# The attention branch's projection of an encoder layer as seven block products for each pair of column tiles

## The chip, the core and the metric

The kernel runs on one core of one Trainium2 chip. The metric is the device time of one execution in microseconds (us). Three runs of the kernel before gave 2049.7, 2049.95 and 2050.43 us; the median is 2049.95. The engines are TensorE (PE; its weight loads are listed as PEld), VectorE (DVE), ScalarE (ACT), GpSimd (POOL) and SyncE (SP). POOL and SP issue the transfers here.

## The reference, cut to what matters

One encoder layer on 1024 tokens of 1024 channels: a SwiGLU FFN with a layer norm, a mixer with a layer norm, and a second FFN with a layer norm. The mixer's end is what changes:

```
g_attn = gates[..., :D_MODEL]
g_four = gates[..., D_MODEL:]
merged = g_attn * (attn @ w_proj_attn) + g_four * (four @ w_proj_fourier)
return merged @ w_out
```

`attn` is (1024 tokens, 512), `w_proj_attn` is (512, 1024). The product `attn @ w_proj_attn` is the attention branch's projection.

## The kernel before, in words

**Number format.** A float32 operand x is held as two tiles: hi, x rounded to the matmul's input format by an ACT copy, and lo, x minus hi on DVE (`split`, L352; the two instructions are L358 and L363). A product takes three matmuls, hi·hi, hi·lo and lo·hi (`TERMS`), into one PSUM bank of 128x512 float32. There are eight banks. SBUF pages are 128x1024 float32, 46 of them; half pages 128x512, eleven.

**Seven block products.** The large products of the kernel are done in 2x2 blocks with seven block products instead of eight. With the operand's blocks a11 to a22 and the weight's b11 to b22 the kernel forms

```
s1 = a21 - a22   s3 = a11 - a21   s2 = s1 - a11   s4 = a12 + s2
t1 = b11 + b12   t2 = t1 + b22    t3 = b12 + b22  t4 = t2 + b21
PROD = {1: ("a11", "b11"), 2: ("a12", "b21"), 3: ("s4", "b22"), 4: ("a22", "t4"),
        5: ("s1", "t1"), 6: ("s2", "t2"), 7: ("s3", "t3")}
```

Class `Operand` (L411) holds an operand's blocks: `derive` makes the sums on DVE (L473, L476, L479, L482) and splits each of the seven left factors; `mms` (L492) issues a block product's matmuls. A block product with four inner tiles is twelve matmuls. The banks are shared: bank A collects products 1 and 2, bank B begins as a copy of A after product 1 and collects 6, 7 and 4, bank D collects 5 and 3. Between the products ACT copies B away and DVE forms differences, so that the four output blocks come out of three banks.

**The plan.** Class `Flow` orders the whole kernel when it is built. `job` gives PE's work in a fixed order, each with a cost from `MM = 0.2267` us for one matmul of 128x512. `V`, `S` and `G` are DVE, ACT and POOL steps with costs, a job that needs them and a lead; `Q` are loads; `F` are small PE floats that are put between jobs when they are ready. `Flow.run` walks through the jobs and gives each engine's next instruction by these costs, by due times and by free banks and pages. What comes out is one fixed order for each engine; on the chip, semaphores keep the order between engines, and each engine works in its own order.

**The stage around the change** comes between the gate products (the last pairs `s20` and `s21`, PE line L495, tiles As and Ds) and the output projection (`WJ`, L2214, tiles wA, wB, wD). It holds:

- the four attention tiles of 128 inner rows by 1024 tokens, stored by `combine` (L1870) in `attn_d`, loaded into `at` (L1943, SP) and split into `ap0` to `ap3`;
- the projection `PJ[c]` for eight column tiles c (`run`, L2125, tile pj): four inner tiles by three terms by two halves of tokens, 24 matmuls into two banks, then on DVE the product with the gate tile `gl` out of both banks (L2133);
- the weights `wpa`, prepared and stored earlier by `keep_parts` (L1751; loads L1806), loaded again as hi and lo at L1778;
- the Fourier branch: channel products `fc` (L1965), their parts `fold` (L1976 on ACT, L1981 on DVE), position sums `fse`, `fp`, `fsem`, `fpm` (L2035, L2006, L2067), from whose banks the parts are taken on ACT and DVE: sine halves `fsp` (L2049, L2053), cosine parts `fch` and `fcl` (L2013 to L2019), edge terms `f_se` (L2024, L2025), middle terms `fmidT` (the same lines with four rows, and L2076), the middle weights `wm` (L2097 on ACT, L2098 on DVE); then `FJ[c]` for eight column tiles (L2151 to L2159, tiles pfe, pfo, pfs; three banks each), after which ACT takes the sine half `pfq` (L2166) and DVE forms the outputs (L2173 to L2177), the product with the gate (L2180) and the sum with the attention branch (L2189, tile ma), which is the output projection's operand `M` (`X4`).

The order of PE's jobs is given by `branch_jobs` (L1729): PJ 0 to 4, FJ 0 and 1, PJ 5, FJ 2 and 3, PJ 6, FJ 4 and 5, the first output-projection job, FJ 6, PJ 7, FJ 7, and the rest of the output projection.

Of the kernel before, what the change touches and what calls it, by code (L numbers as in the profile page):

```python
# [12 lines left out]
AF = mybir.ActivationFunctionType  # L13
# [3 lines left out]
P = 128  # L17
S0 = 1024
D = 1024
# [55 lines left out]
class Flow:  # L75
# [232 lines left out]
def kernel(  # L308
# [14 lines left out]
    def as_k(t, kd=KD):  # L323
        return t.rearrange("p (k n) -> p k n", k=kd)
# [86 lines left out]
    class Operand:  # L411


        def __init__(self, name):
            self.name = name
            self.raw, self.part, self.node, self.got = {}, {}, {}, {}

        def cols(self, n, kind, k):
            return pick(self.part[n, k // 2], kind)[:, (k % 2) * 512:(k % 2) * 512 + 512]

        def nodes(self, n):
            return [self.node[n, i] for i in range(2)]

        def turn(self, m, node, tile_of, c0, slack=4.0):

# [27 lines left out]
        def derive(self, first, whole, lead):  # L453

            raw, got = self.raw, self.got

            def parts(n, i, deps, need, src=None, gives=0, tokens=False):
                self.node[n, i] = split(f"{self.name}{n}{i}", lambda: raw[src or n, i],
                                        lambda p: self.part.__setitem__((n, i), p), deps, need,
                                        lead if need is first.get(n) else 14.0, gives=gives, tokens=tokens)  # L460
                return self.node[n, i]
            for n in ("a11", "a12", "a21", "a22"):
                for i in range(2 if first[n] else 0):
# [6 lines left out]
            for i in range(2):  # L470
# [12 lines left out]
                v1 = V(1.23, s1, got["a21", i] + got["a22", i], whole[6], lead + 6, 6.0, pages=1)  # L483
                v3 = V(1.23, s3, [v1, self.node.get(("a21", i), [])] + list(got["a11", i]), whole[6], lead + 5, 5.0)
                v2 = V(1.23, s2, [v3, self.node["a11", i]], whole[6], lead + 4, 4.0)
                parts("s2", i, [v2], whole[6], "a11", 1)
                parts("s3", i, [v3], whole[7], "a21", 1)
                parts("s1", i, [v1], whole[5], None, 2)
                v4 = V(1.23, s4, [v2, self.node["a12", i]], whole[3], lead + 3, 3.0)
                parts("s4", i, [v4], whole[3], "a12", 1)  # L490

        def mms(self, out, w, xn, first, last):  # L492
            for k in range(4):
                for ti, (a, b) in enumerate(TERMS):
                    nc.tensor.matmul(out, pick(w, a)[:, k * P:(k + 1) * P], self.cols(xn, b, k),  # L495
                                     start=first and k == 0 and ti == 0, stop=last and k == 3 and ti == 2,
                                     skip_group_check=True)


# [1226 lines left out]


    PJ, FJ, WJ = {}, {}, {}
    def branch_jobs(attn_, four_):  # L1729
        for c in attn_:  # L1730
            PJ[c] = job(24 * MM, None, 2, gives=(2 if c % 2 else 0) + (8 if c == 7 else 0))
        for c in four_:
            FJ[c] = job(3.1, None, 3, gives=(2 if c % 2 else 0) + (8 if c == 7 else 0))
    branch_jobs((0, 1, 2, 3, 4), (0, 1))
    branch_jobs((5,), (2, 3))
    branch_jobs((6,), (4, 5))
    WORDER = ((1, "A", True), (2, "A", False), (6, "B", False), (7, "B", False), (5, "D", True), (4, "B", False),
              (3, "D", False))
    for p, bk, new in WORDER:
        for m in range(4):  # L1740
            WJ[p, m] = job(12 * MM, None, int(new), gives=8 if m == 3 else 0)
            if (p, m) == (1, 0):
                branch_jobs((), (6,))
                branch_jobs((7,), (7,))

    root_table(FJ[0])


# [53 lines left out]
    for c2 in range(4):  # L1802
        cs = slice(c2 * 256, (c2 + 1) * 256)

        def load_pa(t, cs=cs):
            nc.sync.dma_start(as_k(t, 4), w_pa.rearrange("(k p) n -> p k n", p=P)[:, :, cs])  # L1806
# [61 lines left out]
    attn = {}  # L1868

    def combine(h):  # L1870

# [41 lines left out]
        for hf in range(2):  # L1913
# [25 lines left out]
            T["n", hf] = an  # L1939

        def load():
            T["a"] = t = page(f"at{h}")
            nc.sync.dma_start(t, attn_d[h])  # L1943
        q = Q(PJ[0], 0.5, load, [(T["n", 0], 5.0), (T["n", 1], 5.0)], 26.0, pages=1)
        split(f"ap{h}", lambda: T["a"], lambda p: attn.__setitem__(h, p), [q], PJ[0], 30.0)

    for h in range(SLOTS):
        combine(h)
# [161 lines left out]
        return Q(need, 0.5, run, [(gate_n[w, c], 5.0)], pages=1)  # L2110

    pj_n, seeds = {}, {}
    for c in range(8):
        c2, cc = divmod(c, 2)
        st = {}
        if cc == 0:
            kept["a", c2](("a", c2), PJ[c], 28.0)

        def run(c=c, c2=c2, cc=cc, st=st):
            st["b"] = bk = [bank(f"pj{c}{hf}") for hf in range(2)]  # L2120
            wv = [as_k(t, 4) for t in PW["a", c2]]
            for k in range(4):
                for ti, (a, b) in enumerate(TERMS):
                    for hf in range(2):
                        nc.tensor.matmul(bk[hf], pick(wv, a)[:, k, cc * P:(cc + 1) * P],  # L2125
                                         pick(attn[k], b)[:, hf * 512:(hf + 1) * 512],
                                         start=(k == 0 and ti == 0), stop=(k == 3 and ti == 2))
        PJ[c].fn = run
        q = gate_load(0, c, PJ[c])

        def mul(hf, c=c, st=st):
            t = gates[0, c][:, hf * 512:(hf + 1) * 512]
            nc.vector.tensor_mul(t, t, st["b"][hf])  # L2133
        pj_n[c] = [V(0.69, lambda hf=hf, mul=mul: mul(hf), [PJ[c], q], frees=1) for hf in range(2)]

    for c in range(8):
        c2, cc = divmod(c, 2)
        st = {}
# [25 lines left out]
        def sine(c=c, st=st):  # L2164
            st["q"] = half(f"pfq{c}")
            nc.scalar.activation(st["q"], st["s"], AF.Copy)  # L2166
            if c > 5:
                seeds[c - 6][0] = st["s"]

        def outs(c=c, st=st):  # L2170
            pe, po, q = st["e"], st["o"], st["q"]
# [19 lines left out]
        n = S(0.62, sine, [FJ[c]], frees=int(c < 6), halves=1)  # L2191
        if c > 5:
            seeds[c - 6] = [None, n]
        n = V(1.8, outs, [n], frees=2, hgives=1, pages=1)
        n = V(1.23, gate, [n, q], gives=1)
        n = V(1.38, merge, [n] + pj_n[c], gives=2, pages=2 if cc == 0 else 0)
        for r in (1, 2):
            X4.got.setdefault((f"a{r}{c // 4 + 1}", c % 4 // 2), []).append(n)

# [189 lines left out]
```

## Time and profile before

| what | value |
|---|---|
| median of three runs | 2049.95 us (2049.7 to 2050.43) |
| profiled execution: span from the first to the last instruction | 2048.2 us |
| what lies around the span, median less span | 1.75 us |
| instructions | 25801 |
| from the first pj matmul to the end of FJ 7 | 1255.7 to 1342.1 us |
| DMA moved over the whole span | 442.23 MB |

The profiled execution lists no time of its own beside its span; the median of the runs stands for it. In the profile's lists a group names line, engine, operation, written tile and read tiles; "x24" is a count. In a timeline the columns are start, length, engine, line, operation, tiles, shape, and in brackets how long the engine had been idle before it and what ended the idle time. The matmuls of a timeline overlap, so that the distance between starts, not the length, is what one costs. The chain that ended last is followed back from the last instruction. A list of waits gives the waiting engine and line, what it waited for, the sum, the count and the longest.

### The profile page before, as it was taken

How to read it: one execution, taken by the hardware profiler on the slowest of the kernel's cores; microseconds unless marked ns; L12 is line 12 of the kernel's file. 1: busy time of each engine (PE TensorE's matmuls, PEld its weight loads, DVE VectorE, ACT ScalarE, POOL GpSimd, SP SyncE). 2: the span in 40 equal slices, each digit the busy share in tenths (PEclk: the TensorE clock that was granted, in tenths of full speed). 3: DMA queues.
4: the chain of work that ended last, by engine and by line, in shares of the span. 5: the costliest groups of instructions: out<-in, count | busy, mean ns of one | idle time of the engine just before them, and what ended most of it. 6: DMA issues, size and time to landing. Idle time of an engine off the chain costs nothing.

```text
span 2048.2 us, 25801 instructions
## 1 busy us (share of the span) xinstructions
PE 2037.5 (99%) x9411; PEld 1700.3 (83%) x9411; DVE 1339.6 (65%) x1930; ACT 893.6 (44%) x1417; POOL 266.9 (13%) x464
## 2 busy tenths in 40 slices
PE   9999999999999999999999999999999999999998
PEld 7888888888888888888888888888888888888886
DVE  7765555576685668665656664777876665575565
ACT  6433333454453224665556443236633333355332
POOL 0122211111001122231121110000011111110000
PEclk9999999999999999999999999999999999999999
DMA  5778875599856566564455659574257886658752
GB/s 206 237 236 259 257 230 148 171 339 402 291 189 187 178 228 212 195 207 147 117 142 169 232 209 373 183 297 175 78 179 238 272 243 205 194 205 292 238 184 94
DMA packets 164144, 442.23 MB, mean 216 GB/s; under 512 B 20370, under 2 KB 42722, under 8 KB 163504
## 3 DMA queue, kind: packets, MB, share of 16 engines
q1 hardware_dynamic: 118928, 288.41, 40.7%
q0 software_dynamic: 45088, 152.16, 25.1%
q8 instruction: 74, 1.21, 0.2%
q14 instruction: 54, 0.44, 0.1%
HBM read 329.63 MB, written 176.91 MB: 247 GB/s over the span
## 4 chain that ended last, share of the span: by engine, by line
PE 98%; DMA 1%; ACT 1%; DVE 0%; issue 0%; SPq 0%; DVEq 0%
PE Ab L495 14%; PE Aa L495 14%; PE Aq L495 8%; PE Db L495 6%; PE Da L495 6%; PE As L495 5%; PE Dq L495 3%; PE Xb L864 3%; PE Xa L864 3%; PE Zb L864 3%; PE Za L864 3%; PE pj L2125 2%; PE v L1291 2%; PE Ds L495 2%; PE wA L2214 2%; PE vB L1230 2%
## 5 line engine op out<-in xcount | busy, mean ns | idle before, releaser
L1621 ACT ACTIVATE p<-p,stat 128x192 f32<-128x192 f32 (+2 forms) x96 | 42.2, 441 | 29.7 <-DVE stat L1616 27.7
L338 POOL DMA_DIRECT2D hsaa<-t2a x21 | 12.0, 569 | 316.0 <-DVE t2a L730 297.9
L338 POOL DMA_DIRECT2D n_spill<-y x16 | 9.0, 565 | 297.5 <-DVE y L1061 297.5
L338 POOL DMA_DIRECT2D hsba<-t2b x21 | 11.6, 550 | 265.4 <-DVE t2b L730 253.6
L726 DVE TENSOR_TENSOR t2a<-Da,t2a 128x512 f32<-128x512 f32 x21 | 14.5, 691 | 45.2 <-PE Da L495 45.2
L633 ACT ACTIVATE t2b<-Ab 128x512 f32<-128x512 f32 x21 | 12.6, 598 | 63.8 <-PE Ab L495 63.8
L726 DVE TENSOR_TENSOR t2b<-Db,t2b 128x512 f32<-128x512 f32 x21 | 14.5, 691 | 39.1 <-PE Db L495 39.1
L633 ACT ACTIVATE t2a<-Aa 128x512 f32<-128x512 f32 x21 | 12.5, 598 | 62.5 <-PE Aa L495 62.5
L1411 DVE SCALAR_TENSOR_TENSOR oq<-Dq,b_cols,t2q 128x512 f32<-128x512 f32 x12 | 11.8, 985 | 41.2 <-PE Dq L495 41.2
L1606 DVE SCALAR_TENSOR_TENSOR p<-sc,bias 128x512 f32<-128x512 f32 (+1 forms) x40 | 24.4, 619 | 17.9 <-PE sc L1592 17.6
L1667 PEld LDWEIGHTS pv<-pT,v 128*128 128x128 f32 x240 | 32.4, 191 | 3.3 <-ACT pT L1646 1.0
L1592 PE MATMUL sc<-oq,oq 128*128 128x192 f32 (+2 forms) x192 | 34.4, 322 | 0.0
L718 DVE TENSOR_TENSOR t3a<-Da,t3a 128x512 f32<-128x512 f32 x21 | 14.5, 690 | 29.2 <-PE Da L495 25.2
L1667 PE MATMUL pv<-pT,v 128*128 128x128 f32 x240 | 32.8, 275 | 0.6 <-ACT pT L1646 0.6
L1592 PEld LDWEIGHTS sc<-oq,oq 128*128 128x128 f32 x192 | 29.5, 190 | 1.7
L495 PE MATMUL Da<-Xs40h,usa 128*128 128x512 f32 x84 | 29.3, 389 | 0.0
L495 PE MATMUL Da<-Xs41h,usa 128*128 128x512 f32 x84 | 29.3, 389 | 0.0
L495 PE MATMUL Db<-Zs40h,usb 128*128 128x512 f32 x84 | 29.3, 389 | 0.0
L495 PE MATMUL Db<-Zs41h,usb 128*128 128x512 f32 x84 | 29.3, 389 | 0.0
L718 DVE TENSOR_TENSOR t3b<-Db,t3b 128x512 f32<-128x512 f32 x21 | 14.5, 690 | 22.1 <-PE Db L495 20.0
L1411 DVE SCALAR_TENSOR_TENSOR oq<-Dq,b_cols,t3q 128x512 f32<-128x512 f32 x12 | 11.9, 991 | 22.9 <-PE Dq L495 18.8
L1046 ACT ACTIVATE y<-ya,lsa 128x1024 f32<-128x1024 f32 x8 | 9.1, 1143 | 35.7 <-DVE lsa L1041 35.7
(7481 smaller groups left out, 7318.9 us busy)
## 6 DMA issues: line engine op xcount, KB each, us to landing
qa<-hsas SPq DMA_DIRECT2D x43, 256.0 KB, 5.9
qa<-tdat SPq DMA_DIRECT2D x43, 256.0 KB, 5.4
qb<-hsbs SPq DMA_DIRECT2D x43, 256.0 KB, 4.0
ga<-in_ffn_gu_dram SPq DMA_DIRECT2D x21, 512.0 KB, 6.3
ua<-in_ffn_gu_dram SPq DMA_DIRECT2D x21, 512.0 KB, 7.8
gb<-in_ffn_gu_dram SPq DMA_DIRECT2D x21, 512.0 KB, 4.6
ub<-in_ffn_gu_dram SPq DMA_DIRECT2D x21, 512.0 KB, 6.8
qb<-tdbt SPq DMA_DIRECT2D x33, 256.0 KB, 4.3
```

The costliest lines, as they stand in the source:

```text
L338: nc.gpsimd.dma_start(*a, **kw)
L495: nc.tensor.matmul(out, pick(w, a)[:, k * P:(k + 1) * P], self.cols(xn, b, k), start=first and k == 0 and ti == 0, stop=last and k == 3 an ...
L718: nc.vector.tensor_sub(H[c, "t3"], B[c, "D"], H[c, "t3"])
L726: nc.vector.tensor_sub(H[c, "t2"], B.pop((c, "D")), H[c, "t2"])
L864: nc.tensor.matmul(bank_, a, b, start=first and ti == 0, stop=last and ti == len(todo) - 1, skip_group_check=True)
L1230: nc.tensor.matmul(B["v", bk, m], X2.cols(xn, a, k)[:, m * P:(m + 1) * P], pick(w, b), start=new and k == 0 and ti == 0, stop=k == 3 and t ...
L1291: nc.tensor.matmul(ps, X2.cols(f"a{hf + 1}{k // 4 + 1}", a, k % 4)[:, mm * P:(mm + 1) * P], pick(wv, b), start=(k == 0 and ti == 0), stop= ...
L1592: nc.tensor.matmul(sv[:, i, :], qk[0][:, qt * P:(qt + 1) * P], qk[1][:, k0:k0 + w], start=True, stop=True, skip_group_check=True)
L1621: nc.scalar.activation(p3()[:, i, :], p3()[:, i, :], AF.Exp, bias=stats[h][:, k, 0:1], scale=1.0, accum_out=stats[h][:, k, 1:2])
L1667: nc.tensor.matmul(bk[:, at:at + P], env["v"][kc, rows], pt[:, sl * P:(sl + 1) * P], start=not split_ and qt not in seen, stop=last, skip_ ...
L2125: nc.tensor.matmul(bk[hf], pick(wv, a)[:, k, cc * P:(cc + 1) * P], pick(attn[k], b)[:, hf * 512:(hf + 1) * 512], start=(k == 0 and ti == 0 ...
L2214: nc.tensor.matmul(B["w", bk, m], X4.cols(xn, a, k)[:, m * P:(m + 1) * P], pick(w, b), start=new and k == 0 and ti == 0, stop=k == 3 and t ...
```

## The change

The projection of the attention branch is done in seven block products as well, for each of four pairs of column tiles. The inner 512 rows and the 1024 tokens are cut in halves: a block of the operand has two inner tiles of 128 rows and 512 tokens and is one page (`Operand("T", 1)`), a block product is six matmuls (`PJ[c2, p]`, pair c2, product p).

- The attention tiles are loaded as four blocks (`attn_loads`), summed and split by `derive` into seven left factors.
- For each pair there are besides the weight tile `wpa` the sums `wpt` (t1 to t4): loaded in the first FFN at pairs 12, 14, 16 and 18, summed on DVE (`sum_pa`), split, stored and loaded again in the stage. `load_pa` takes two column tiles one after the other.
- `branch_pair` makes a pair's products and the steps between them: ACT copies A into B (`seed`), keeps B after products 6 and 7 (`keep`), DVE forms D less a kept B (`less`) and the gate products out of A, B and the differences (`mul`). Product 2 waits for the copy of A, product 7 and product 4 for a kept B, product 3 for the difference of D. Pairs 2 and 3 use the sine banks of FJ 0 and FJ 3 as B.
- The order of PE's jobs is new: the fourteen products of pairs 0 and 1 mixed, then FJ 0; those of pairs 2 and 3 in ones, twos and threes between FJ 1 to FJ 7. The sums with the Fourier branch are declared after all pairs.

```diff
-        def __init__(self, name):
-            self.name = name
+        def __init__(self, name, pages=2):
+            self.name, self.pages = name, pages
...
         def mms(self, out, w, xn, first, last):
-            for k in range(4):
+            kt = 2 * self.pages
+            for k in range(kt):
...
-        for c in attn_:
-            PJ[c] = job(24 * MM, None, 2, gives=(2 if c % 2 else 0) + (8 if c == 7 else 0))
+        for c2, p in attn_:
+            PJ[c2, p] = job(6 * MM, None, {1: 1 if c2 in SINE else 2, 5: 1}.get(p, 0),
+                            gives=(2 if p in (3, 4) else 0) + (2 if c2 == 3 else 0))
...
-    branch_jobs((0, 1, 2, 3, 4), (0, 1))
-    branch_jobs((5,), (2, 3))
-    branch_jobs((6,), (4, 5))
+    branch_jobs([(0, 1), (1, 1), (0, 6), (0, 2), (1, 6), (0, 7), (1, 2), (0, 5), (1, 7), (0, 4), (1, 5), (0, 3), (1, 4), (1, 3)], (0,))
+    branch_jobs([(2, 1)], (1,))
+    branch_jobs([(2, 6), (2, 2)], (2,))
+    branch_jobs([(2, 7), (2, 5)], (3,))
+    branch_jobs([(2, 4), (2, 3), (3, 1)], (4,))
+    branch_jobs([(3, 6), (3, 2)], (5,))
...
-                branch_jobs((), (6,))
-                branch_jobs((7,), (7,))
+                branch_jobs([(3, 7), (3, 5)], (6,))
+                branch_jobs([(3, 4), (3, 3)], (7,))
...
+        def sum_pa(w, raw):
+            to, b = as_k(w, 4), as_k(raw, 4)
+            nc.vector.tensor_add(to[:, 0:4:2], b[:, 0:4:3], b[:, 2:3].to_broadcast([P, 2, 256]))
+            nc.vector.tensor_add(to[:, 1], to[:, 0], b[:, 3])
+            nc.vector.tensor_add(to[:, 3], to[:, 1], b[:, 1])
...
+        kept["t", c2] = keep_parts(f"wpt{c2}", load_pa, [], sum_pa, early=J[("a", 12 + 2 * c2), 4])
...
+    def branch_pair(c2):
+        bk, at = {}, lambda p: PJ[c2, p]
...
+        for p in PROD:
+            def run(p=p):
+                if p == 1:
+                    bk["A"] = bank(f"pA{c2}")
+                    if c2 not in SINE:
+                        bk["B"] = bank(f"pB{c2}")
+                if p == 5:
+                    bk["D"] = bank(f"pD{c2}")
+                XB.mms(bk[BANK[p]], W.pop((("t", c2), PROD[p][1])), PROD[p][0], p in (1, 5), True)
+            at(p).fn = run
+            at(p).after(XB.nodes(PROD[p][0]))
...
+        n1 = S(0.62, seed, [at(1)] + ([sines[SINE[c2]][1]] if c2 in SINE else []), at(6), tail=0.4)
+        at(2).after(n1)
+        n2 = S(0.62, keep("t2"), [at(6)], at(7), halves=1)
+        n3 = S(0.62, keep("t3"), [at(7)], at(4), halves=1)
+        o11 = V(0.69, mul(0, L, "A"), [at(2), q[0]], frees=1)
+        u1 = V(0.69, less("t3"), [at(5), n3], at(3))
+        m1 = V(0.69, mul(1, R, "t3"), [u1, q[1]], hgives=1)
+        o21 = V(0.69, mul(0, R, "B"), [at(4), q[0]], frees=1)
+        u0 = V(0.69, less("t2"), [at(3), n2], frees=1)
+        m0 = V(0.69, mul(1, L, "t2"), [u0, q[1]], hgives=1)
```

More of the change, by code (lines that the diff above doesn't have):

```diff
@@ L421, in nodes @@
         def nodes(self, n):
-            return [self.node[n, i] for i in range(2)]
+            return [self.node[n, i] for i in range(self.pages)]
         def turn(self, m, node, tile_of, c0, slack=4.0):
@@ L462, in derive @@
             for n in ("a11", "a12", "a21", "a22"):
-                for i in range(2 if first[n] else 0):
+                for i in range(self.pages if first[n] else 0):
                     if isinstance(got[n, i], tuple):
@@ L469, in derive @@
                         parts(n, i, got[n, i], first[n])
-            for i in range(2):
+            for i in range(self.pages):
                 def s1(i=i):
@@ L492, in mms @@
         def mms(self, out, w, xn, first, last):
-            for k in range(4):
+            kt = 2 * self.pages
+            for k in range(kt):
                 for ti, (a, b) in enumerate(TERMS):
                     nc.tensor.matmul(out, pick(w, a)[:, k * P:(k + 1) * P], self.cols(xn, b, k),
-                                     start=first and k == 0 and ti == 0, stop=last and k == 3 and ti == 2,
+                                     start=first and k == 0 and ti == 0, stop=last and k == kt - 1 and ti == 2,
                                      skip_group_check=True)
@@ L1728 @@
     PJ, FJ, WJ = {}, {}, {}
+    XB = Operand("T", 1)
+    SINE = {2: 0, 3: 3}
     def branch_jobs(attn_, four_):
-        for c in attn_:
-            PJ[c] = job(24 * MM, None, 2, gives=(2 if c % 2 else 0) + (8 if c == 7 else 0))
+        for c2, p in attn_:
+            PJ[c2, p] = job(6 * MM, None, {1: 1 if c2 in SINE else 2, 5: 1}.get(p, 0),
+                            gives=(2 if p in (3, 4) else 0) + (2 if c2 == 3 else 0))
         for c in four_:
             FJ[c] = job(3.1, None, 3, gives=(2 if c % 2 else 0) + (8 if c == 7 else 0))
-    branch_jobs((0, 1, 2, 3, 4), (0, 1))
-    branch_jobs((5,), (2, 3))
-    branch_jobs((6,), (4, 5))
+    branch_jobs([(0, 1), (1, 1), (0, 6), (0, 2), (1, 6), (0, 7), (1, 2), (0, 5), (1, 7), (0, 4), (1, 5), (0, 3), (1, 4), (1, 3)], (0,))
[4 more added lines that the diff above has]
+    branch_jobs([(3, 6), (3, 2)], (5,))
     WORDER = ((1, "A", True), (2, "A", False), (6, "B", False), (7, "B", False), (5, "D", True), (4, "B", False),
@@ L1742 @@
             if (p, m) == (1, 0):
-                branch_jobs((), (6,))
-                branch_jobs((7,), (7,))
+                branch_jobs([(3, 7), (3, 5)], (6,))
+                branch_jobs([(3, 4), (3, 3)], (7,))
+    PJ[0], PJ[1], PJ[2] = PJ[0, 1], PJ[0, 5], PJ[0, 7]
     root_table(FJ[0])
@@ L1803, with load_pa @@
         cs = slice(c2 * 256, (c2 + 1) * 256)
-        def load_pa(t, cs=cs):
-            nc.sync.dma_start(as_k(t, 4), w_pa.rearrange("(k p) n -> p k n", p=P)[:, :, cs])
+        def load_pa(t, c2=c2):
+            for i in range(2):
+                ns = slice((2 * c2 + i) * P, (2 * c2 + i + 1) * P)
+                nc.sync.dma_start(as_k(t[:, i * 512:(i + 1) * 512], 4), w_pa.rearrange("(k p) n -> p k n", p=P)[:, :, ns])
         def load_pf(t, cs=cs):
@@ L1867 @@
     attn_d = [kb.dram([P, S0], f"attn_d{h}") for h in range(SLOTS)]
-    attn = {}
+    attn_n = {}
     def combine(h):
@@ L1938, in combine @@
             fl.later(an, 4.0, hgives=1)
[L1939 to L1945, printed above, removed]
+            attn_n[h, hf] = an
     for h in range(SLOTS):
@@ L2112, with attn_loads, load @@
     pj_n, seeds = {}, {}
[L2113 to L2134, printed above, removed]
+    def attn_loads():
+        for r in range(2):
+            for q in range(2):
+                n = f"a{r + 1}{q + 1}"
+                def load(n=n, r=r, q=q):
+                    XB.raw[n, 0] = t = page(f"T{n}")
+                    for i in range(2):
+                        nc.sync.dma_start(t[:, i * 512:(i + 1) * 512], attn_d[2 * q + i][:, r * 512:(r + 1) * 512])
+                XB.got[n, 0] = [Q(PJ[0], 0.5, load, [(attn_n[2 * q + i, r], 5.0) for i in range(2)], 26.0, pages=1)]
@@ new lines, with names, run, seed @@
+    attn_loads()
+    XB.derive({"a11": PJ[0, 1], "a12": PJ[0, 2], "a21": None, "a22": PJ[0, 4]}, {p: PJ[0, p] for p in PROD}, 30.0)
+    def branch_pair(c2):
+        bk, at = {}, lambda p: PJ[c2, p]
+        def names(key, places):
+            def run(t):
+                for n, i in places:
+                    W[("t", c2), n] = tuple(x[:, i * 256:(i + 1) * 256] for x in t)
+            kept[key, c2]((key, c2), at(1) if key == "a" else at(6), 22.0, run)
+        names("a", (("b11", 0), ("b21", 1), ("b22", 3)))
+        names("t", (("t1", 0), ("t2", 1), ("t3", 2), ("t4", 3)))
+        for p in PROD:
[9 more added lines that the diff above has]
+            at(p).after(XB.nodes(PROD[p][0]))
+        q = [gate_load(0, 2 * c2 + i, at(2) if i == 0 else at(5)) for i in range(2)]
+        def seed():
+            if c2 in SINE:
+                bk["B"] = sines[SINE[c2]][0]
+            nc.scalar.activation(bk["B"], bk["A"], AF.Copy)
+        def keep(t):
+            def run():
+                bk[t] = half(f"p{t}{c2}")
+                nc.scalar.activation(bk[t], bk["B"], AF.Copy)
+            return run
+        def less(t):
+            def run():
+                nc.vector.tensor_sub(bk[t], bk["D"], bk[t])
+            return run
+        def mul(i, cs, t):
+            def run():
+                g = gates[0, 2 * c2 + i][:, cs]
+                nc.vector.tensor_mul(g, g, bk.pop(t))
+            return run
+        n1 = S(0.62, seed, [at(1)] + ([sines[SINE[c2]][1]] if c2 in SINE else []), at(6), tail=0.4)
[8 more added lines that the diff above has]
+        m0 = V(0.69, mul(1, L, "t2"), [u0, q[1]], hgives=1)
+        pj_n[2 * c2], pj_n[2 * c2 + 1] = [o11, o21], [m1, m0]
@@ L2136 @@
+    sines, four_out = {}, {}
     for c in range(8):
@@ L2166, in sine @@
             nc.scalar.activation(st["q"], st["s"], AF.Copy)
-            if c > 5:
-                seeds[c - 6][0] = st["s"]
+            for keep_ in (seeds[c - 6],) if c > 5 else (sines[c],):
+                keep_[0] = st["s"]
         def outs(c=c, st=st):
@@ L2190 @@
         q = gate_load(1, c, FJ[c])
-        n = S(0.62, sine, [FJ[c]], frees=int(c < 6), halves=1)
-        if c > 5:
-            seeds[c - 6] = [None, n]
+        n = S(0.62, sine, [FJ[c]], frees=int(c < 6 and c not in SINE.values()), halves=1)
+        (seeds if c > 5 else sines)[c - 6 if c > 5 else c] = [None, n]
         n = V(1.8, outs, [n], frees=2, hgives=1, pages=1)
-        n = V(1.23, gate, [n, q], gives=1)
-        n = V(1.38, merge, [n] + pj_n[c], gives=2, pages=2 if cc == 0 else 0)
+        four_out[c] = V(1.23, gate, [n, q], gives=1), merge
+    for c2 in range(4):
+        branch_pair(c2)
+    for c in range(8):
+        n, merge = four_out[c]
+        n = V(1.38, merge, [n] + pj_n[c], gives=2, pages=2 if c % 2 == 0 else 0)
         for r in (1, 2):
```

## The prediction, made before the result was known

> **What bounds the kernel now.** I read the page's busy shares first, then the chain that ended last, then who TensorE (PE) waited for.
>
> ```profile
> span 2048.2 us, 25801 instructions
> PE 2037.5 (99%) x9411; PEld 1700.3 (83%) x9411; DVE 1339.6 (65%) x1930; ACT 893.6 (44%) x1417; POOL 266.9 (13%) x464
> PE 98%; DMA 1%; ACT 1%; DVE 0%; issue 0%; SPq 0%; DVEq 0%
> ```
>
> ```profile
> PE warm L2293 <- DVE eps L334: 1.4, 1, 1.4
> PE pv L1667 <- ACT pT L1646: 0.6, 1, 0.6
> PE Aa L495 <- DVE Xa110l L392: 0.2, 1, 0.2
> PE Aa L495 <- DVE Xa111l L392: 0.2, 1, 0.2
> ```
>
> PE is busy for 99% of the span, the chain is PE for 98%, and all of PE's waits on other engines come to 2.4 us, none of them in the stage that changes. So a matmul less is its issue time less, as long as nothing new makes PE wait. The question is what one matmul costs and which new waits open. The chain in that stage, in order of time (start, length, what):
>
> ```profile
> 1277.22 5.47 PE pj L2125 x24
> 1282.69 0.34 PE fse L2035 x4
> 1283.03 2.97 PE fp L2006 x24
> 1286.01 0.17 PE fsem L2067 x4
> 1286.18 1.47 PE fpm L2006 x12
> 1287.65 10.90 PE pj L2125 x48
> ```
>
> 48 projection matmuls of 128x512 follow one another in 10.90 us: 0.2270 us each. Eight column tiles take 24 each, 192 in all, with no gap.
>
> **The change part by part.** *Removed from PE.* I write P(c2,p) for the block product p of column pair c2, F(c) and W(p,m) for the Fourier and output-projection jobs. Four pairs times seven products times six matmuls (two inner tiles, three terms) are 168, of the same shape. The order of the built program shows nothing else that moves on PE but the small fc, fse and fp groups among these products. 24 matmuls less are 24 x 0.2270 = **5.45 us**.
>
> The Trainium skill's page "TensorE: Matmul & The Clock Gate", section "Back-to-back issue gap", gives about 131 ns for a matmul of 512 in a sustained stream of weight loads and matmuls, so its estimate of the saving would be 3.1 us. The row above measures 227 ns, and the sum goes by the row.
>
> *The new wait.* Before, a projection tile reads only operands that stand ready. Now each pair's products share banks: A (P1, P2), B (a copy of A, then P6, P7, P4) and D (P5, P3). ScalarE (ACT) copies B ahead of P2 and P7 and P4, and VectorE (DVE) must take D minus a kept B before P3 adds to D. So P3 waits for a subtraction that stands in DVE's queue. For pair 1 the built program puts it behind the whole tail of the Fourier preparation. On PE the order is: first fp group, fsem and fpm, P(1,7), P(0,4), second fse and fp, P(1,5), P(0,3), P(1,4), P(1,3). On DVE: first group's parts, the fmid parts, product with P(0,4), wm, second group's parts, then the subtraction. The same steps in the profile of before (PE, ACT, DVE in order of time: start, length):
>
> ```profile
> 1255.69 0.62 PE L2125 MATMUL pj<-ap0h,wpa0h 128*128 128x512 f32 x2
> ...
> 1277.06 0.63 PE L2125 MATMUL pj<-ap0h,wpa1h 128*128 128x512 f32 x2
> 1277.32 0.60 ACT L2049 ACTIVATE fsp<-fp 128x512 fp32r<-128x512 f32 x1 [3.01 <-PE fp L2006]
> ```
>
> ```profile
> 1250.45 0.69 DVE L1417 TENSOR_TENSOR t3s<-Ds,t3s 128x512 f32<-128x512 f32 x1
> ...
> 1278.21 0.35 DVE L2014 SCALAR_TENSOR_TENSOR fcl<-fp,f_se,fch 128x128 fp32r<-128x128 f32 x1 [3.19 <-ACT fch L2013]
> ...
> 1280.41 0.68 DVE L2053 TENSOR_TENSOR fsp<-fp,fsp 128x512 fp32r<-128x512 f32 x1
> ...
> 1289.20 0.69 DVE L2053 TENSOR_TENSOR fsp<-fp,fsp 128x512 fp32r<-128x512 f32 x1
> 1289.81 0.14 DVE L2024 COPY f_se<-fsem 4x2 f32<-4x2 f32 x1
> ...
> 1290.44 0.34 DVE L2014 SCALAR_TENSOR_TENSOR fmidT<-fpm,f_se,fmidT 4x128 fp32r<-4x128 f32 x1 [0.32 <-ACT fmidT L2013]
> ...
> 1293.24 1.22 DVE L2098 TENSOR_TENSOR wm<-wmr,wm 4x1024 fp32r<-4x1024 f32 x1
> 1294.48 1.28 DVE L2133 TENSOR_TENSOR gl<-gl,pj 128x512 f32<-128x512 f32 x2
> ```
>
> From the end of the first fp group (ACT starts on it at 1277.32, call that 0) DVE needs: to fsp 3.09 (1277.32 to 1280.41); fsp to f_se 0.61; the fmid parts up to wm 3.43 (1289.81 to 1293.24); the product with P(0,4), new here, 0.60 (half of the pair of 1.28, less overlap); wm 1.24; f_se to the first fcl 0.63 (1289.81 to 1290.44); fcl to the next free slot 2.20 (1278.21 to 1280.41); the subtraction 0.69, as the same form at 1250.45. Sum 12.49. PE, whose next job started at 1277.06, that is at -0.26, reaches P(1,3) after fsem and fpm 1.64, two products of 1.36 (6 x 0.227), fse and fp 3.31, three products 4.08: -0.26 + 1.64 + 2.72 + 3.31 + 4.08 = 11.49. **PE waits 1.0 us.** Nothing behind hides it, since PE is the bound. The row shows none of this order itself, so both ends: nothing if DVE's steps close up by 1.0, and 2.5 if the ACT steps between them (fch, fmid, wm) each start half a microsecond late. I take the sum, 1.0. Behind the subtraction DVE has the second sine part, needed only in F(0) some 4 us later.
>
> *The other new waits, at nothing.* The first copy of A into B starts when ACT is free:
>
> ```profile
> 1256.61 0.72 ACT L1422 ACTIVATE os<-t2s,b_cols 128x512 f32<-128x512 f32 x1 [2.75 <-DVE t2s L1417]
> ...
> 1301.65 0.60 ACT L2166 ACTIVATE pfq<-pfs 128x512 f32<-128x512 f32 x1 [8.73 <-PE pfs L2159]
> ...
> 1304.71 0.60 ACT L2166 ACTIVATE pfq<-pfs 128x512 f32<-128x512 f32 x1 [0.94 <-PE pfs L2159]
> ```
>
> It goes behind the os row, from about 1257.2 to 1257.8; P(0,6) starts two products after 1255.69, at 1258.4. Spare 0.6. All other copies have a product or an F job beside them (spare 1.6 and more); pairs 2 and 3 have F jobs between their steps, 3.06 long (F(0) and F(1) follow each other, and their sine halves are fetched at 1301.65 and 1304.71), so their subtractions come some 3 us early.
>
> *More work on DVE and ACT.* Seven operand splits in place of four, four sums and differences of 1024 columns, four keeps or seeds and two subtractions more per pair. Where DVE is dense is from F(0) on. A column costs it 3.99 (1302.28 to 1306.27):
>
> ```profile
> 1302.28 0.43 DVE L2173 TENSOR_TENSOR prf<-pfe,pfq 128x256 f32<-128x256 f32 x1 [2.63 <-ACT pfq L2166]
> ...
> 1306.27 0.42 DVE L2173 TENSOR_TENSOR prf<-pfe,pfq 128x256 f32<-128x256 f32 x1
> ...
> 1347.99 1.22 DVE L363 TENSOR_TENSOR Ma121l<-ma,Ma121h 128x1024 fp32r<-128x1024 f32 x1
> ```
>
> ```profile
> 1342.11 0.60 ACT L2166 ACTIVATE pfq<-pfs 128x512 f32<-128x512 f32 x1 [6.05 <-PE pfs L2159]
> ```
>
> From F(0) to F(7) PE now has 8 x 3.06 + 14 x 1.36 + 2.72 = 46.2 us; until it can start on F(7), DVE has seven columns, 27.9, twelve steps of 0.60 for pairs 2 and 3, 7.2, and four of 1.22 for W's operands (as Ma121l), 4.9: 40.0 in the 43.1 that remain after F(0). It fits with 3.1 to spare. Behind F(7) the chain is as before: 1342.11 to the end of Ma121l at 1349.21, 7.1 us, against 36 W matmuls and half a W job, 9.5, ahead of its first use. Spare 2.4 less what DVE is behind. I take nothing.
>
> *Weight sums.* Each t-weight (three adds, one split, two stores of 512 KB, loads of 512 KB) is made in the first FFN, one per 38 us, where DVE is busy for 27 of 50 us:
>
> ```profile
> 250.00:300.00 50.00, 50.00 (x222) 41.42 (x221) 27.45 (x36) 15.90 (x22) 7.04 (x12) 1.00 0.87 263
> 1225.00:1260.00 35.00, 35.00 (x157) 28.96 (x156) 18.42 (x21) 16.15 (x21) 4.23 (x7) 1.00 0.83 314
> 1260.00:1290.00 30.00, 30.00 (x201) 26.94 (x200) 13.40 (x41) 6.31 (x16) 1.53 (x3) 1.00 0.97 375
> ```
>
> (PE, PEld, DVE, ACT, POOL busy, clock, DMA share, GB/s.) Their 1.5 MB per 38 us are 40 GB/s on 263 at a share of 0.87, which just fills the queues; the cover is the lead of the gate and up weights, and I cost it at nothing, at worst 3 us.
>
> *Transfers into the stage.* Four loads of 1 MB are new, two of them early. The DMA queue's own rows and landings:
>
> ```profile
> 1230.03 0.33 SPq L1778 DMA_DIRECT2D wpa0h<-wpa_d  x1
> ...
> 1252.74 0.32 SPq L1778 DMA_DIRECT2D wpa2h<-wpa_d  x1
> ...
> 1257.85 0.32 SPq L1778 DMA_DIRECT2D wpf0l<-wpf_d  x1
> ```
>
> ```profile
> wpa0h<-wpa_d SPq DMA_DIRECT2D x1, 512.0 KB, 3.6
> DMA packets 164144, 442.23 MB, mean 216 GB/s; under 512 B 20370, under 2 KB 42722, under 8 KB 163504
> ```
>
> When the queue is full, 512 KB go in 1.28 us (four from 1252.74 to 1257.85). Up to the last half of the second t-weight there are now 17 such pieces from 1230.0 (four of attn, eight of weights, one gate tile, two position tables, two gate stores): 21.8 + 2.3 for landing, 1254; P(1,6) first reads it at 1261. Spare 7; the first t-weight, two pieces earlier and read from 1258.4, has as much. I cost it at nothing.
>
> *Sum.* -5.45 + 1.0 = -4.45 us. The profiled execution's span goes from 2048.2 to 2043.75; the median of the runs shown lies 1.75 above the span, which stays: **2045.5 us**, 0.22% less than 2049.95.
>
> **The rivals.**
> *No new wait* (DVE closes up its fmid and cosine steps): 2049.95 - 5.45 = 2044.5. For it: before, PE's waits were nil here though DVE did the same steps. Against it: those had 10.9 us of pj behind them, now 5.4.
> *A second wait beside the first*, at the 0.6 of spare at P(0,6), at W's Ma121l, or in the first FFN: 1 to 4 us more, 2046.5 to 2049.5, centre 2047.3. For it: several spares of 0.6 to 2 us against starts known to some tenths; the pv row above shows PE waiting 0.6 for one ACT step. Against it: nowhere else in before.
> *The change doesn't save what it says*: in before, two neighbouring matmuls read the same weights, and if that made them cheaper, the seven-product form would cost more for each. If half the saving went that way, each of the 168 would take 0.2432 (43.58 less 2.72, over 168), and 2.72 less 1.0 leaves 2048.2. Against it: the chain of the gate products, which never share weights, runs at the same pace:
>
> ```profile
> 1239.98 7.71 PE As L495 x34
> ```
>
> 7.71 / 34 = 0.2268. The page of the Trainium skill named above would end beside this rival: by its 131 ns, 3.1 saved and 1.0 lost, an estimate of 2047.9 us; the trace doesn't agree with its figure.
> *Slower: the t-weights land late.* 17 pieces at the mean rate of the whole span, 216 GB/s, take 41.3 us instead of 21.8: landing at 1273.6, P(1,6) 12 us late; -5.45 + 12 + 1.0 gives 2057.5. It decides from about 240 GB/s down (landing at 1270, 8.6 us late, cancels the saving and 0.2% more). For it: a DMA share of 0.97 in that stretch. Against it: the queue moved 410 GB/s there when full. The same page of the Trainium skill, section "HAM oscillation — how this bites in real kernels", says that a PE gap of over about 3.4 us halves the clock afterwards, which by its estimate would add some 2 us to this rival; no row here has such a gap.
>
> **How the numbers follow.** 0.2% is 4.1 us, about what a measurement can tell from no change. Forecast 0.45, no new wait 0.10: both faster by more, 0.55. A second wait 0.33 and smaller saving 0.05: within 0.2%, 0.38. Late weights 0.07: slower. The range leaves out the slower case and the upper third of the second wait: 2044.2 to 2048.4.
>
> **What would show it.** 168 matmuls at 0.227 in the stage; one PE wait on DVE of about 1.0 before P(1,3) and no other over 0.3; the same pace in W and after; DVE with short idle times between F(0) and F(7); t-weights landed by 1256. A PE wait on ACT at P(0,6), on a DMA at P(0,6) or P(1,6), or on DVE at W(2,0), would make it wrong; so would new PE waits at 180 to 330 us.

## The result and the profile after

The changed kernel takes 2046.76 us (median of 20 runs, 2046.15 to 2048.42), the kernel before 2050.24 in the same series (20 runs, 2049.70 to 2051.65). The ratio is 0.9983, 95% interval 0.9977 to 0.9990: 3.5 us less, between 2.0 and 4.7. The interval leaves out 1, so the kernel is faster, but by 0.17%, less than the 0.2% from which the forecast counted a kernel as faster. 2045.5 had been forecast: the gain was to be 4.45 us and is 3.5. The time lies in the forecast's range (2044.2 to 2048.4). Of its classes it was not the likelier one that came (faster by more than 0.2%, 0.55), but the next (within 0.2%, 0.38).

The page of the changed kernel, and PE's waits (engine, line, what it waited for, sum, count, longest):

```profile
span 2044.8 us, 25909 instructions
PE 2033.2 (99%) x9387; PEld 1695.7 (83%) x9387; DVE 1363.2 (67%) x1961; ACT 907.1 (44%) x1436; POOL 271.5 (13%) x472
```

```profile
PE pD L496 <- DVE pt L2175: 0.9, 1, 0.9
PE Ds L496 <- DVE t3s L1418: 0.6, 1, 0.6
```

24 matmuls fewer (9411 less 9387), PE still at 99%. Two waits are new. The first is the forecast one, P(1,3) on a subtraction. The second was not forecast: the last gate product (tile Ds) waits for VectorE's t3s before the changed stage has begun.

Waits alone don't add up to the missing time, so I measure the way from one PE instruction to another. Three marks are the same in both kernels: the first matmul As<-Ya220h,t34s20h in the gate products, the first matmul of the projection, and the long run of 84 output-projection matmuls behind F(7). Before (timeline of PE, then the chain; the projection's first matmul, 1255.69, stands in the prediction):

```profile
1231.21 0.39 PE L495 MATMUL As<-Ya220h,t34s20h 128*128 128x512 f32 x1
```

```profile
1342.07 19.04 PE wA L2214 x84
```

After (timeline of PE; then the chain in order of time, whose columns are start, length, what):

```profile
1231.42 0.39 PE L496 MATMUL As<-Ya220h,t34s20h 128*128 128x512 f32 x1
...
1253.15 0.39 PE L496 MATMUL As<-Ya221h,t34s21l 128*128 128x512 f32 x1
1254.16 0.50 PE L496 MATMUL Ds<-Ys40h,uss 128*128 128x512 f32 x1 [0.63 <-DVE t3s L1418]
...
1257.02 0.39 PE L496 MATMUL pA<-Ta110h,wpa0h 128*128 128x512 f32 x1
...
1290.02 0.39 PE L496 MATMUL pB<-Ta220h,wpt1l 128*128 128x512 f32 x1
1291.29 0.50 PE L496 MATMUL pD<-Ts40h,wpa1h 128*128 128x512 f32 x1 [0.89 <-DVE pt L2175]
```

```profile
1240.56 0.73 ACT os L1423
...
1241.58 7.24 DMA gate_d<-os
1248.92 1.07 ACT posp0h L358
1250.01 0.68 DVE posp0l L363
...
1251.15 0.41 DVE Ta220l L363
...
1252.29 0.25 DVE Ta L482
...
1253.42 0.69 DVE t3s L1418
...
1339.19 19.04 PE wA L2277 x84
```

| stretch of PE | before | after | difference |
|---|---|---|---|
| gate products: As<-Ya220h to the first projection matmul | 24.48 | 25.60 | +1.12 |
| stage: from there to the long W run | 86.38 | 82.17 | -4.21 |
| both | 110.86 | 107.77 | -3.09 |

Each such time comes from one profiled execution. The span fell by 3.4. The other 0.3 is +0.21 that was there before the first mark and -0.52 behind the W run. The first is there already in the first FFN, ahead of every new step (a run of 36 Aa matmuls starts at 48.52 before and at 48.75 after; the first load for the weight sums goes out at 171.58). In the six experiments below the first mark lies anywhere from 1230.92 to 1232.02, and from the W run to the end of the span they have 705.6 to 705.7 us, as the changed kernel has (705.61; before 706.13); in the fifth of them the projection is the old one. So neither difference is put down to the change. What it does lies between the marks: in the stage 5.45 of matmuls were to go and 4.21 went; ahead of it 1.12 were lost where nothing had been forecast.

Read the chain from below to see how. The last gate product stands until t3s is done at 1254.1. That subtraction stands on VectorE behind three steps: posp0l, which is the Fourier branch's position table and was there before the change, and two of the new operand, Ta220l and the sum Ta. posp0l stands behind ScalarE's posp0h, and posp0h behind the store gate_d<-os, 7.24 us from issue to landing. A store whose data nothing here waits for holds PE up: an output tile of the gate lies in an SBUF page until it has been stored, and posp0h had been given that page. The order of ScalarE is new too. After, then before (timelines):

```profile
1248.92 1.06 ACT L358 ACTIVATE posp0h<-pos 128x1024 fp32r<-128x1024 f32 x1 [2.26 <-DMA gate_d<-os]
1249.88 0.58 ACT L634 ACTIVATE t3s<-As 128x512 f32<-128x512 f32 x1
```

```profile
1247.73 0.60 ACT L633 ACTIVATE t3s<-As 128x512 f32<-128x512 f32 x1 [1.08 <-PE As L495]
...
1249.17 1.05 ACT L358 ACTIVATE posp0h<-pos 128x1024 fp32r<-128x1024 f32 x1
```

Before, both engines had t3s ahead of the position table (on VectorE t3s at 1250.45 and posp0l at 1251.06); now both have it behind.

### The profile page after: what moved, and what is told of

It reads as the page before. It is cut to its first block, busy times and chain, and to the rows that moved or that the text cites. A ratio compares the mean times of both kernels' runs of the same rounds, so it can differ in the third digit from the quotient of the medians.

```text
span 2044.8 us, 25909 instructions
## 1 busy us (share of the span) xinstructions
PE 2033.2 (99%) x9387; PEld 1695.7 (83%) x9387; DVE 1363.2 (67%) x1961; ACT 907.1 (44%) x1436; POOL 271.5 (13%) x472
## 4 chain that ended last, share of the span: by engine, by line
PE 97%; DMA 1%; ACT 1%; DVE 1%; issue 0%; SPq 0%; DVEq 0%; ACTq 0%
PE Ab L496 14%; PE Aa L496 14%; PE Aq L496 8%; PE Db L496 6%; PE Da L496 6%; PE As L496 4%; PE Dq L496 3%; PE Xb L865 3%; PE Zb L865 3%; PE Za L865 3%; PE Xa L865 3%; PE v L1292 2%; PE wA L2277 2%; PE Ds L496 2%; PE vB L1231 2%; PE Va L865 1%
```

## The experiments

**Theory.** The matmuls save their full 5.45. The changed kernel gives back 1.1 to 1.2 at P(1,3), where VectorE's row of steps is too long, and 1.1 ahead of the stage, where ScalarE stands behind a page that a store still holds. **Rivals:** the matmuls save less than that; the weight sums made in the first FFN cost something; the seven splits are too much for ScalarE and VectorE whatever page they get. In the expectations "stage" is the whole way from As<-Ya220h to the W run, the row "both" of the table; in the text below them it is the row "stage".

### A. The position tables loaded later

```
-        q = Q(PJ[0], 0.5, load, (), 22.0 - i, pages=1)
+        q = Q(PJ[0], 0.5, load, (), 18.0 - i, pages=1)
```

> The changed kernel with the two position tables loaded 4 us later (lead 18 instead of 22), so that the page that posp0h waits for is another one, and no split stands behind the landing of the gate_d store. I measure the stage from the first matmul As<-Ya220h,t34s20h to the start of the long W run: 110.86 us before (1231.21 to 1342.07), 107.77 after (1231.42 to 1339.19). Theory (the changed kernel loses 1.1 us ahead of the stage because ScalarE stands 2.26 us behind a page that a store still holds): ScalarE has no wait on gate_d<-os, the gate products run on with no PE wait on t3s, and the first projection matmul comes 24.6 us after As<-Ya220h instead of 25.6; stage 106.2 to 106.8, total about 1 us below the changed kernel. Rival (the seven splits are simply too much for ScalarE and VectorE there, whatever page they use): t3s stays late, the waits stay at 0.6, stage 107.8.

PE's marks, its new waits, and ScalarE (timeline):

```profile
1231.41 0.39 PE L496 MATMUL As<-Ya220h,t34s20h 128*128 128x512 f32 x1
...
1255.89 0.39 PE L496 MATMUL pA<-Ta110h,wpa0h 128*128 128x512 f32 x1
```

```profile
PE pB L496 <- DMA wpt1l<-wpt_d: 0.7, 1, 0.7
...
PE pB L496 <- DMA wpt1h<-wpt_d: 0.3, 1, 0.3
```

```profile
1247.39 1.06 ACT L358 ACTIVATE Ts20h<-Ta 128x1024 fp32r<-128x1024 f32 x1 [1.49 <-DVE Ta L479]
1248.36 0.58 ACT L634 ACTIVATE t3s<-As 128x512 f32<-128x512 f32 x1
```

24.48 us ahead of the stage, to the hundredth what the kernel before has: the whole loss is gone, with the same seven splits on both engines. ScalarE no longer waits for a store, and t3s is copied at 1248.36 instead of 1249.88. The rival of the seven splits falls. But the edit changed more than the page. Both engines now have t3s ahead of the position table again (posp0h at 1253.96, posp0l at 1255.04), so A can't tell the page from the order. The loads changed places too: the second t-weight now goes out behind the four uc tiles, the input of the Fourier branch, and lands late, and P(1,6) waits 1.0 us for it. By that the stage takes 82.52 (the W run starts at 1338.41), both together 107.00, just outside the 106.2 to 106.8 expected. No wait is listed at P(1,3); F shows why. The time, 2047.12 us (2046.02 to 2049.68, 11 runs, ratio 0.9987, 0.9978 to 0.9996), cannot be told from the changed kernel's and did not show the "about 1 us" expected. The profiled execution is the fastest of the eleven (2046.02), so that the gain ahead of the stage is shown by this one trace alone.

### B. P(1,4) and P(1,3) behind F(0)

```
-    branch_jobs([(0, 1), (1, 1), (0, 6), (0, 2), (1, 6), (0, 7), (1, 2), (0, 5), (1, 7), (0, 4), (1, 5), (0, 3), (1, 4), (1, 3)], (0,))
-    branch_jobs([(2, 1)], (1,))
+    branch_jobs([(0, 1), (1, 1), (0, 6), (0, 2), (1, 6), (0, 7), (1, 2), (0, 5), (1, 7), (0, 4), (1, 5), (0, 3)], (0,))
+    branch_jobs([(1, 4), (1, 3), (2, 1)], (1,))
```

> The changed kernel with P(1,4) and P(1,3) moved behind F(0), so that nothing of pair 1 asks for its second subtraction before F(0). Theory (PE waits for VectorE's whole row of steps up to the second cosine parts, and the subtraction is only its last member): the wait goes from P(1,3) to the first matmul of F(0), which reads fch, 0.8 to 1.0 instead of 0.9; stage 107.5 to 107.8, the time that of the changed kernel within 0.3 us. Rival (it is the subtraction's place in the queue alone): the wait goes, stage 106.6, 1.2 us less.

ScalarE and PE (timelines):

```profile
1249.89 1.06 ACT L358 ACTIVATE posp0h<-pos 128x1024 fp32r<-128x1024 f32 x1 [3.22 <-DMA gate_d<-os]
```

```profile
1291.58 0.36 PE L2210 MATMUL pfe<-fch,wpf0h 128*128 128x258 f32 x1 [0.84 <-DVE fch L2030]
```

The wait moved with the place: 0.84 in F(0), at its seventh matmul and not at its first, instead of 0.89 at P(1,3), and the stage is 82.08 (from 1258.03 to the W run at 1340.11) instead of 82.17. Moving the product that waits gains nothing, because what comes in its place asks the same queue. That the sum is 108.09 and not at most 107.8 comes from ahead of the stage: 26.01 (the first mark is at 1232.02) instead of 25.60, and there the gate store held ScalarE for 3.22 instead of 2.26. The time was 2047.52 us (2046.50 to 2048.39, 11 runs, ratio 0.9986, 0.9977 to 0.9995), 0.8 above the changed kernel's median where 0.3 at most was expected.

### C. Without the low half of wm

```
         nc.scalar.activation(w, raw, AF.Copy)
-        nc.vector.tensor_sub(w[32:36], raw[32:36], w[32:36].bitcast(F32))
```

> The changed kernel without the VectorE subtraction that makes the low half of wm (4 rows, 1.22 us): the Fourier middle row's low-order weight term is left out. All else stands in the same order. Theory (VectorE's row of steps, 12.5 us long, sets P(1,3)): the wait before P(1,3) falls from 0.9 to below 0.1, stage 106.5 to 106.7, 1.1 to 1.2 us less. Rival (ScalarE's steps fch, fsp set it and VectorE only follows): the wait stays over 0.5, stage 107.3 or more.

PE (timeline, then the chain):

```profile
1290.59 0.49 PE L496 MATMUL pD<-Ts40h,wpa1h 128*128 128x512 f32 x1
```

```profile
1338.48 19.04 PE wA L2276 x84
```

The wait before P(1,3) has left the list; all that remains is a first matmul of 0.49 in place of 0.39. The stage takes 81.09 (from 1257.39), 1.08 less than in the changed kernel, for a step of 1.22 us taken from VectorE. So VectorE's row of steps is what PE waits for, and that wait, listed as 0.9, costs 1.1. The sum, 106.97, is 0.3 above what was expected, again ahead of the stage (25.88, from 1231.51). The time was 2046.15 us (2045.55 to 2046.70, 11 runs, ratio 0.9980, 0.9971 to 0.9989).

### D. Four products issued twice

```
-                XB.mms(bk[BANK[p]], W.pop((("t", c2), PROD[p][1])), PROD[p][0], p in (1, 5), True)
+                w_ = W.pop((("t", c2), PROD[p][1]))
+                XB.mms(bk[BANK[p]], w_, PROD[p][0], p in (1, 5), True)
+                if c2 > 1 and p in (6, 4):
+                    XB.mms(bk[BANK[p]], w_, PROD[p][0], False, True)
```

> The changed kernel with P(2,6), P(2,4), P(3,6) and P(3,4) issued twice, 24 matmuls of 128x512 more, which brings PE to as many as before the change; the doubled products are added twice. Theory (each is 0.227 us and PE is the bound): stage 107.77 + 5.45 = 113.2, total 5.4 to 5.5 above the changed kernel and about 2 above before. Rival (24 matmuls are worth less, 131 to 200 ns each): 3.1 to 4.8 us more, stage 110.9 to 112.6.

PE (timeline, then the chain):

```profile
1256.66 0.39 PE L496 MATMUL pA<-Ta110h,wpa0h 128*128 128x512 f32 x1
```

```profile
1344.28 19.04 PE wA L2280 x84
```

The stage takes 87.62, 5.45 more for 24 matmuls: 0.227 us each. The rival of the smaller saving falls. The time, 2052.33 us (2051.47 to 2053.16, 11 runs, ratio 1.0011, 1.0002 to 1.0020), is 5.6 above the changed kernel's and 2.05 above that of before in the same series (2050.28): with as many matmuls as before, the new form costs about 2 us. The marks put it into the two losses, 1.24 each (25.72 ahead of the stage, from 1230.94, and 87.62 in it, against 24.48 and 86.38 before).

### E. Before, with the weight sums only

The loads, adds, split and stores of the four weight sums were added to the kernel before, at the changed kernel's places.

```
+        def load_pt(t, c2=c2):
...
+        def sum_pa(w, raw):
...
+        keep_parts(f"wpt{c2}", load_pt, [], sum_pa, early=J[("a", 12 + 2 * c2), 4])
```

> The kernel before, plus only the making of the weight sums in the first FFN: loads, three adds, split and two stores for each of four column pairs, at the places that the changed kernel has them; the sums are never read back and the projection is the old one. Theory (these steps lie in the cover of the first FFN): no new PE wait over 0.2 us from 130 to 420 us, the distance from the start of the Aa run at 48.5 to the start of the Ta run at 387.3 stays 338.74 us, time that of before within 0.5 us. Rival (they cost part of what is missing from the saving): 0.5 to 3 us more.

Two rows of PE's chain: in the kernel before they start at 48.52 and 387.26.

```profile
48.39 8.16 PE Aa L495 x36
```

```profile
387.13 10.88 PE Ta L495 x48
```

338.74 us in both, to the hundredth, though the DMA share from 180 to 230 us rises from 0.95 to 0.99. The time is 2049.88 against 2050.22 (ratio 0.9998, 0.9988 to 1.0007). By the marks making the sums costs nothing; the rival falls.

### F. The position tables split later

```
-                                  [q], PJ[1], 26.0)
+                                  [q], PJ[1], 12.0)
```

> The changed kernel with the splits of the two position tables asked for 14 us later (lead 12 instead of 26); the loads stay. By the built order the split Ts20h now stands where posp0h stood and takes the same page. Theory (the page that a gate_d store still holds stops ScalarE, whichever split asks for it): ScalarE still has a wait of 2 us or more on gate_d<-os, now before Ts20h, and t3s is copied as late as before (1249.9 in the changed kernel); on VectorE Ta220l no longer stands behind posp0l, so the wait before the last gate product falls from 0.6 to below 0.2, and ahead of the stage 0.2 to 0.4 us are lost instead of 1.12. VectorE has one split more before the second cosine parts or less, so the wait before P(1,3) is 0.2 to 0.6. Stage 106.4 to 107.0. Rival (posp0h itself, through the late landing of its table, was the cause): no wait on gate_d<-os, t3s at 1247.7, nothing lost ahead of the stage.

ScalarE, VectorE and PE (timelines):

```profile
1248.35 1.06 ACT L358 ACTIVATE Ts20h<-Ta 128x1024 fp32r<-128x1024 f32 x1 [2.50 <-DMA gate_d<-os]
```

```profile
1251.72 0.69 DVE L1418 TENSOR_TENSOR t3s<-Ds,t3s 128x512 f32<-128x512 f32 x1
```

```profile
1230.92 0.39 PE L496 MATMUL As<-Ya220h,t34s20h 128*128 128x512 f32 x1
...
1255.57 0.39 PE L496 MATMUL pA<-Ta110h,wpa0h 128*128 128x512 f32 x1
```

```profile
1337.10 19.04 PE wA L2277 x84
```

Another split now stands in posp0h's place, and ScalarE waits for the same store, for 2.50 us. So what holds ScalarE is the page, whichever split asks for it, and t3s is copied as late as before, at 1249.32, 18.40 behind the first mark (18.46 in the changed kernel). Yet ahead of the stage PE takes 24.65: 0.17 is lost instead of 1.12. VectorE made the difference, in the changed kernel and in F (timelines):

```profile
1250.01 1.22 DVE L363 TENSOR_TENSOR posp0l<-pos,posp0h 128x1024 fp32r<-128x1024 f32 x1 [1.23 <-ACT posp0h L358]
```

```profile
1249.44 1.23 DVE L363 TENSOR_TENSOR Ts20l<-Ta,Ts20h 128x1024 fp32r<-128x1024 f32 x1 [0.33 <-ACT Ts20h L358]
```

In the changed kernel VectorE's next step was posp0l, and VectorE stood still for 1.23 us until ScalarE had made its other half. In F Ta220l goes first, whose other half is ready, and VectorE stands still for 0.33; t3s comes at 1251.72 instead of 1253.42. So in F the held page costs PE 0.17 at most. In the changed kernel it cost 1.12 together with an order that put a step waiting for it ahead of t3s on VectorE as well. No run frees the page and keeps the order.

The wait at P(1,3) is gone too, but not because VectorE became quicker: the edit moved PE's order as well. The Fourier branch's first position sums (fp) now come two products earlier, so that P(1,2) and P(0,5) stand between them and P(1,3) (PE, the first matmuls of P(1,2) and of P(1,3)):

```profile
1276.44 0.40 PE L496 MATMUL pA<-Ta120h,wpa1h 128*128 128x512 f32 x1
...
1289.34 0.39 PE L496 MATMUL pD<-Ts40h,wpa1h 128*128 128x512 f32 x1
```

From ScalarE's start on the first fp group (1275.05) PE reaches P(1,3) after 14.29 us instead of 11.58, and VectorE's subtraction, behind a longer row, ends after 13.94 instead of 12.57. A has the same order and nearly the same numbers (14.29 and 13.93). The stage takes 81.53; a wait listed as 0.3 for the second t-weight is left. Both make 106.18, 1.6 us less than the changed kernel and a little better than expected. F has the lowest median of all: 2045.41 us (2044.72 to 2047.13, 11 runs), 4.8 less than before in the same series (2050.22), ratio 0.9978 (0.9969 to 0.9987). It is faster than before beyond the noise. The changed kernel's interval (0.9977 to 0.9990) overlaps with F's, so that the 1.35 us between their medians, from two series, rest on the marks.

## Why the forecast was close and where it failed

**The matmuls, -5.45: right.** Experiment D adds 24 and measures 5.45, and in the changed kernel a product of six takes 1.36 (P(0,1) from 1257.02 to 1258.38), 0.227 each, as in the old projection. The 131 ns that the Trainium skill's page "TensorE: Matmul & The Clock Gate", section "Back-to-back issue gap", gives for one is not what these matmuls cost; D says 227 ns.

**The wait at P(1,3), 1.0: right in place, cause and size.** ScalarE and VectorE in the changed kernel:

```profile
1278.67 0.60 ACT L2061 ACTIVATE fsp<-fp 128x512 fp32r<-128x512 f32 x1 [4.37 <-PE fp L2018]
```

```profile
1281.78 0.69 DVE L2065 TENSOR_TENSOR fsp<-fp,fsp 128x512 fp32r<-128x512 f32 x1
1282.38 0.14 DVE L2036 COPY f_se<-fsem 4x2 f32<-4x2 f32 x1
...
1285.75 0.69 DVE L2181 TENSOR_TENSOR gl<-gl,pB 128x512 f32<-128x512 f32 x1
1286.47 1.22 DVE L2110 TENSOR_TENSOR wm<-wmr,wm 4x1024 fp32r<-4x1024 f32 x1
1287.72 0.16 DVE L2036 COPY f_se<-fse 128x2 f32<-128x2 f32 x1
...
1288.34 0.35 DVE L2026 SCALAR_TENSOR_TENSOR fcl<-fp,f_se,fch 128x128 fp32r<-128x128 f32 x1 [0.28 <-ACT fch L2025]
...
1290.55 0.69 DVE L2175 TENSOR_TENSOR pt<-pD,pt 128x512 f32<-128x512 f32 x1
```

From 1278.67 the steps take, one row's start to the next, 3.11, 0.60, 3.37, 0.72, 1.25, 0.62, 2.21 and 0.69, in sum 12.57; the forecast had 3.09, 0.61, 3.43, 0.60, 1.24, 0.63, 2.20 and 0.69, in sum 12.49. PE was there at 11.58 (1290.02 + 0.23 - 1278.67), forecast 11.49. Here a queue whose steps and order were known was worked out to a tenth from the other kernel's trace. Experiment C shows that it is this row, and B that its end, not the subtraction, is what counts. The loss, 1.08, is a little more than the forecast wait.

**"More work on DVE and ACT", taken at nothing: the step that failed.** Busy times of the changed kernel (stretch, length, then PE, PEld, DVE, ACT and POOL, clock, DMA share, GB/s), from F(0)'s columns to the W run and ahead of the stage:

```profile
1296.60:1338.80 42.20, 42.20 (x233) 36.83 (x232) 37.57 (x70) 12.35 (x19) 0.00 (x0) 1.00 0.83 306
1230.00:1257.00 27.00, 26.37 (x115) 21.27 (x115) 18.73 (x20) 14.83 (x19) 3.67 (x6) 1.00 0.95 344
```

The forecast looked for VectorE being dense from F(0) on, and there it was right: 37.57 us of 42.20, and PE never waits. It counted the splits, but it did not follow the two queues ahead of the stage, and that is the step that failed: a term put at nothing which measured 1.12. There VectorE is busy for only 18.73 us of 27 and ScalarE for 14.83, so by their lengths the new splits fit. But each engine goes through one queue, and t3s, on which the last gate product depends, now stands in it behind the position table's split and two steps of the new operand. What those cost is not their length but how long VectorE stands still in front of them, and that was set by a page and by the order (F). "A second wait beside the first" was among the rivals, with a chance of 0.33 and a centre of 2047.3, and the measured 2046.76 lies near it; but its three places (P(0,6), W's Ma121l, the first FFN) were all wrong, so that the time came near this number was luck. The forecast's own signs say the same: no other wait than the one at P(1,3) was to be over 0.3, and the one on t3s is 0.6. P(0,6) did not wait, Ma121l ended 2.2 us ahead of its first use, and experiment E shows the first FFN free.

**Transfers, nothing: right, by less than worked out.** The last half of the second t-weight was to land at 1254:

```profile
1246.42 0.32 SPq L1787 DMA_DIRECT2D wpt1l<-wpt_d  x1
```

```profile
wpt1l<-wpt_d SPq DMA_DIRECT2D x1, 512.0 KB, 12.7
```

It landed 12.7 us after its issue, at 1259.1 and so later than the forecast's sign (by 1256), and P(1,6) read it from 1262.7: spare 3.6, not 7. In A and F, where the four uc tiles go ahead of it, the spare is gone and PE waits 1.0 and 0.3 us. So late t-weights stood nearer than the working said, and an order of loads kept them away; the 12 us of the slower rival no run shows.

**The sum.** Forecast -5.45 + 1.0 = -4.45. Measured between the marks: -5.45, +1.08 (C), +1.12 (A), and 0.16 that is in none of the edits (stage of C, 81.09, less 86.38 - 5.45): -3.09.

## What to carry to other kernels

Where PE is the bound and work is taken from it, look for the new waits also ahead of the edited stage: its new operands are prepared there, in the same in-order queues as the neighbour's steps. For each prepared tile ask not only when its input comes but whose page it takes, when that page's last store lands, and which steps stand behind it in the queue. And price a wait by the whole row of steps in front of it: moving the one instruction that waits (B) gained nothing; taking one step out of the row (C), or giving PE two more products to do while the row runs (A and F), did. When a planner lays out the order, look in the trace for what else an edit has moved: A and F were meant for one table and moved loads, splits and PE's products.

## What the runs showed of the hardware

- A wait costs PE more than its listed time. The one listed as 0.63 began the matmul 0.78 after its turn (1253.15 + 0.23, then 1254.16), that matmul is 0.50 long instead of 0.39, and the next starts 0.34 behind it (1254.50) instead of 0.23. The wait listed as 0.9 cost 1.08 (C); the one listed as 0.6 cost 1.12, together with a smaller one ahead of it for ScalarE's copy of t3s (A).
- The store gate_d<-os of 512 KB lands 7.1 to 8.0 us after its issue in the chains of the changed kernel and A to D, where the DMA share is 0.95 (1230 to 1257, changed kernel). ScalarE is held for 2.26, 3.22, 2.61 and 2.76 us in the changed kernel, B, C and D, and PE loses 1.12, 1.53, 1.40 and 1.24 ahead of the stage, with the same order of steps there.
- The load wpa0h of 512 KB landed 3.6 us after its issue in the kernel before and 9.3 in the changed kernel; wpt1l, as large, took 12.7 there. The landing, not the issue, is what has to be set against the first use.
